# Attention scores from a stationary block that holds a query head's high part above its low part, in float32r, and two small tiles moved to another buffer ring

## The chip, the cores and the metric

The kernel runs on one core of a Trainium2 chip. The metric is device time in microseconds (us) of one execution. Engines are named as in the profile: PE (matrix multiply), DVE (vector), ACT (scalar and activation functions), POOL (GpSimd) and SP (here it only issues transfers). Each engine takes its instructions in the order of the program, and a transfer is issued when SP, POOL or ACT reaches it.

## The reference

Two layers over 256 latent tokens and 256 context tokens of width 1024. Each layer has a token mixer (windowed attention with grouped queries, and a recurrence in two directions called HGRN2, merged by gates and one output projection), then a mixture of experts in which each of 16 experts chooses its tokens. The change is in the scores of the attention:

```python
ATTN_HEADS = 8; ATTN_KV_HEADS = 2; HEAD_DIM = 64; WINDOW = 128; WBLOCK = 128
def window_attention(q, k, v, kc, vc, sink):       # latents: window keys and context keys
    ...
    s_win = jnp.einsum('bntgrd,bnsgd->bngrts', qb, kw).astype(jnp.float32) * scale
    ...
    s_ctx = jnp.einsum('bntgrd,bcgd->bngrtc', qb, kc).astype(jnp.float32) * scale
    ...
def context_attention(q, k, v, sink):              # context rows: context keys alone
    ...
    s = jnp.einsum('btgrd,bsgd->bgrts', qg, k).astype(jnp.float32) * (dh ** -0.5)
```

The latents' two blocks of 128 queries see 512 keys each (256 latents, of which the other block's are masked to the window, and 256 context tokens); the context's two blocks see 256. The context rows are needed in the first layer only. So there are 16 heads of scores against 512 keys and 16 against 256 in the first layer, and 16 against 512 in the second.

## The kernel before

The span has four stages: the mixer of layer 0 (until about 500 us), its experts (first expert at 534.67 us), the mixer of layer 1 (from about 976 us), and its experts (first expert at 1356.00 us, until the end). A framework's scheduler, which simulates the engines, fixes the order of instructions on every engine before the kernel runs. A tile that shares a buffer with an earlier one waits until the earlier one's last reader is done, so the buffers decide part of that order.

Mixers. The large products (input projections, branch products, output products) split each factor into a high and a low float32r part and add three products (`mm3`, L168 to L170); weights come by DMA (`win`, `wbr`, `wo`) and are split by ACT (L478) and by POOL or DVE (L479). Between them on PE stand the pieces of the attention and the recurrence. One head of scores was one float32 product: the stationary side is a query block `qT` of 128 rows (two heads of 64), the moving side is `kT`, four copies of the keys in which the other head's 64 rows are zero. `kT` is filled in `blk_ka` and zeroed in `kv_in`. Each head then goes through a chain of maximum, exponential, scaling, transposes and a product with the values (L704 to L727), on DVE, ACT and PE.

Fillers. The weights that turn the conditioning vector into scales and shifts are 80 tiles of 512 KB and some smaller ones. `mod_steps` makes them in steps: `load` issues a `wmod` transfer on SP (L284, two buffers), `work` multiplies it (four products, L294), and the eighth step of a group copies the result from PSUM to a row tile `mrow` (L247), transposes it (L250) and adds a bias (L254). The scheduler puts these steps into gaps.

Buffers. `T` has a ring of two [128, 512] buffers, taken by `t2(...)`, which small tiles of many kinds use one after the other: `qr`, `kr`, `vr`, `y`, `wraw` and, in the router, `wk`. `mrow` lay in the pool of the `wmod` tiles, of which the experts' pools (`moe_pools`) reuse the space, and the readout's tile `hg` (`hg_out`, L666) in the mixer's pool `C`.

Router. After a layer's mixer the post-norm, then `bcol` (DVE, L1045, after PE L1044), logits (PE L1065), softmax, and per row block `s` eight rounds of maximum and replace on `wk` (DVE, L1082 and L1083), which end in a one-hot tile `OH` (L1102). PE gathers the chosen rows by it (L1136), and the first expert follows (L1218). The experts' weights are 1 MB tiles on SP (L1011).

Of the kernel before, what the change touches and what calls it, by code (L numbers as in the profile page):

```python
# [11 lines left out]
F32 = mybir.dt.float32  # L12
# [97 lines left out]
def tile_kernel(ctx, tc, x, c, ctx_in, c_ctx, w_mod, b_mod, w_in, attn_sink, lb_fw, lb_bw, norm_g,  # L110
                w_br_a, w_br_h, w_out, w_router, w_gate, w_up, w_down, ln_g, ln_b, cst_d, msk_d, out):
    nc = tc.nc
# [165 lines left out]
    def mod_steps(l, q0, ns):  # L278

        state = {}  # L280

        def load(k, md):
            w = md.tile([128, 1024], F32, name="wmod", tag="wmod", bufs=2)
            ins = nc.sync.dma_start(w, _dram(w_mod, l * D * 6 * D + k * 128 * 6 * D + 512 * q0, [[6 * D, 128], [1, 1024]]))  # L284
            if first:
                in_order(first[:], ins)
            state[k] = w

        def work(k, md):
            if k == 0:  # L290
                state["p"] = mdb()
            pm, w = state["p"], state.pop(k)
            for j in range(4):
                mm(pm[32 * j:32 * j + 32, 0:256], scol[:, k, :], w[:, 256 * j:256 * j + 256],  # L294
                   start=(k == 0), stop=(k == KT - 1))
            if k < KT - 1:
                return
            mod_cols(l, pm, md.tile([128, 256], F32, name="mrow", tag="mrow", bufs=1), q0, 1, ns)
        return [(lambda md, k=k: load(k, md), lambda md, k=k: work(k, md)) for k in range(KT)]

    def mcol(l, sec, k, s):
# [122 lines left out]
    def front(l, fillers, X=None, finish=None):  # L424
# [229 lines left out]
        def hg_out(h, A, ihv):  # L654
            AT, A1, A2 = A
            p = ob()
            for t in range(NT):
                s, i = t // 2, t % 2
                terms = [(AT[:, t, :], t), (A1[:, s, i, :], 2 * s + 1 - i)]
                if s == 0:  # L660
                    terms += [(A2[:, j, 128 * i:128 * i + 128], 2 + j) for j in range(2)]
                for n, (a, tv) in enumerate(terms):
                    mm(p[:, 128 * t:128 * t + 128], a, ihv[:, tv, 128 * h:128 * h + 128], start=(n == 0),  # L663
                       stop=(n == len(terms) - 1), skip_group_check=True)
            pv = p[:, :TQ].rearrange("p (t v) -> p t v", v=128)
            hg = C.tile([128, TQ], F32, name="hg")  # L666
            nc.scalar.activation(hg, p[:, :TQ], AF.Square)
            r = T.tile([128, 4], F32, name="hr", tag="hr", bufs=2)[:, :NT]
            hg = hg.rearrange("p (t v) -> p t v", v=128)
            nc.vector.tensor_reduce(r, hg, axis=AX.X, op=ALU.add)  # L670
            nc.vector.tensor_scalar(r, r, 1.0 / 128, EPS, op0=ALU.mult, op1=ALU.add)
            nc.gpsimd.tensor_tensor(r, r, nhalf[:, 0:NT], op=ALU.pow)
            nc.vector.tensor_tensor(hg, pv, r[:, :, None].to_broadcast([128, NT, 128]), op=ALU.mult)
            for t in range(NT):
                nc.tensor.transpose(p[:, 128 * t:128 * t + 128], hg[:, t, :], ident)
            nc.vector.scalar_tensor_tensor(hgT[:, h, :], p[:, :TQ], ng[:, 4 * l + h:4 * l + h + 1], hgT[:, h, :],
                                           op0=ALU.mult, op1=ALU.mult)
# [11 lines left out]
        def attention(s, i2, qT, kT, va):  # L689
# [3 lines left out]
            t = 2 * s + i2  # L693
            tk = slice(128 * t, 128 * t + 128)
            for g in range(2):
                eT = C.tile([128, 4, 4, 128], F32, name="eT")
                for i in range(4):
                    hd = 4 * g + i
                    par = i % 2
                    p = scb()  # L700
                    mm(p[:, :nk], qT[:, hd // 2, tk], kT[:, 2 * g + par, k0:k0 + nk], start=True, stop=True)  # L701
                    if s == 0:
                        kc = 128 * (1 - i2)
                        nc.vector.tensor_tensor(p[:, kc:kc + 128], p[:, kc:kc + 128],  # L704
# [27 lines left out]
        def chains():  # L732
            nonlocal C, kT, va, ihv
            C = pool(sC, f"C{l}")
            kT = C.tile([128, 4, 512], F32, name="kT")
            va = C.tile([128, 4, 128], F32, name="va")
            ihv = C.tile([128, 4, 512], F32, name="ihv")

# [5 lines left out]
        def blk_ka(w, j):  # L744
            p = fm(w, j, 512)
            kr = t2("kr")
            rope(kr[:, 0:256], p[:, 0:256])
            nc.scalar.copy(kr[:, 256:512], p[:, 256:512])
            for g in range(2):
                for h in range(2):  # L750
                    (nc.scalar.copy if h else nc.vector.tensor_copy)(kT[64 * h:64 * h + 64, 2 * g + h, :],
                                                                     kr[64 * g:64 * g + 64, :])

        def blk_va(w, j):
            p = fm(w, j, 512)
# [38 lines left out]
            return A  # L794

        def kv_in():
            nc.gpsimd.memset(kT[64:128, 0:4:2, :], 0.0)
            nc.gpsimd.memset(kT[0:64, 1:4:2, :], 0.0)
            w = cols_tile((O_KA, 256))
            blk_ka(w, 0)  # L800
            blk_va(w, 1)
# [522 lines left out]
    def moe_pools(l, st, S, zones, right=()):  # L1324
# [5 lines left out]
        for z, names in enumerate((right,) + zones if right else zones):  # L1330
            Z = pool(sZ, f"ZR{l}", side="right") if names is right else pool(st, f"Z{l}{z}")
            for n in names:
                if isinstance(n, int):
                    for i in range(n):

                        w = 2304 if z == 2 + (right != ()) else 2048
                        slots.append(lambda Z=Z, i=i, w=w: Z.tile([128, w], F32, name=f"w{i}", tag=f"w{i}")[:, :2048])
                elif n not in shapes:

                    once.append(lambda Z=Z, n=n: Z.tile([128, 2048], F32, name="w" + n, tag=n))  # L1340
# [69 lines left out]
```

## Time and profile before

| | us |
|---|---|
| median of 3 runs | 1810.9 |
| lowest and highest | 1810.57, 1813.97 |
| profiled execution | 1812.94 |
| its span, first to last instruction | 1811.2 |
| PE, DVE, ACT, POOL busy in the span | 1562.6, 677.1, 450.0, 305.1 |
| mean granted clock of PE | 0.927 |

Busy times are sums over the span; what bounds a stage is read from the stage. In rows of the windows view each engine's figure is its busy time in that stretch with the number of its instructions behind it, then PE's granted clock, the share of the 16 DMA engines that was busy, and GB/s. In the chain of work each row is a start, a length, and the engine and line (or the DMA) that the end waited for.

### The profile page before, as it was taken

What the parts mean: (1) busy time and instruction counts of PE and PEld (TensorE: products, weight loads), DVE (VectorE), ACT (ScalarE), POOL (GpSimd) and SP (SyncE); (2) the same over time, 40 slices, a digit from 0 to 9 for tenths busy, and PEclk for the clock granted to TensorE, in tenths of its full rate; (3) what the DMA queues carried; (4) which work ended last, traced back from release to release, by engine and by line L of the source; (5) the groups of instructions that cost most, each with busy time, mean ns of one, the idle gap of its engine ahead of it and who ended that gap; (6) DMA issues with size and microseconds to landing.
All of it is one profiled execution on the core that took longest, in us unless ns stands there. A gap on an engine that the chain in (4) does not pass through costs nothing.

```text
span 1811.2 us, 27388 instructions
## 1 busy us (share of the span) xinstructions
PE 1562.6 (86%) x11342; PEld 925.0 (51%) x11342; DVE 677.1 (37%) x1430; ACT 450.0 (25%) x850; POOL 305.1 (17%) x302
## 2 busy tenths in 40 slices
PE   6999999999989999997998899998968766666666
PEld 4777776688754433332323788775845222322222
DVE  4546566323661221211213756666751100100102
ACT  2436556323120100101000533576410000000000
POOL 2342121123310000000002633331610000000001
PEclk9999999999979999999999999999979777867887
DMA  9644123533679999999999653424689999999997
GB/s 323 186 117 127 60 82 129 177 126 117 245 308 385 421 421 421 421 422 421 421 421 379 208 178 105 130 92 131 241 341 408 421 421 422 420 421 421 421 421 287
DMA packets 159436, 526.06 MB, mean 290 GB/s; under 512 B 9896, under 2 KB 94064, under 8 KB 111184
## 3 DMA queue, kind: packets, MB, share of 16 engines
q1 hardware_dynamic: 157136, 517.46, 74.1%
q0 software_dynamic: 1456, 4.49, 0.7%
q10 hardware_dynamic: 720, 2.36, 0.4%
q8 instruction: 89, 1.46, 0.3%
q14 instruction: 35, 0.29, 0.0%
HBM read 523.23 MB, written 1.05 MB: 289 GB/s over the span
## 4 chain that ended last, share of the span: by engine, by line
PE 53%; DMA 37%; DVE 4%; ACT 2%; POOL 2%; issue 1%; SPq 1%; POOLq 0%; ACTq 0%; DVEq 0%
DMA w<-in_w_up_dram 13%; DMA w<-in_w_down_dram 12%; PE acc L168 9%; DMA w<-in_w_gate_dram 9%; PE acc L170 8%; PE acc L169 8%; PE acc L1218 8%; PE o L1251 4%; DMA wmod<-in_w_mod_dram 3%; PE md L294 2%; PE sc L701 2%; PE sc L724 1%; PE o L663 1%; PE tr L719 1%; PE hs L649 1%
## 5 line engine op out<-in xcount | busy, mean ns | idle before, releaser
L1218 PE MATMUL acc<-w,xs 128*32 128x256 f32 (+1 forms) x3064 | 402.9, 512 | 92.0 <-DMA w<-in_w_up_dram 48.9
L1218 PEld LDWEIGHTS acc<-w,xs 128*32 128x32 f32 (+1 forms) x3064 | 138.0, 130 | 339.2 <-issue 175.9
L1251 PE MATMUL o<-w,hT 128*32 128x256 f32 (+1 forms) x1432 | 188.9, 507 | 44.9 <-DMA w<-in_w_down_dram 30.5
L168 PE MATMUL acc<-uTh,wh 128*128 128x512 f32 (+1 forms) x592 | 215.1, 365 | 3.0 <-ACT qr L682 1.3
L169 PE MATMUL acc<-uTl,wh 128*128 128x512 f32 (+1 forms) x592 | 212.0, 358 | 1.4 <-DVE uTl L398 1.4
L170 PE MATMUL acc<-uTh,wl 128*128 128x512 f32 (+1 forms) x592 | 210.1, 355 | 0.0
L1229 ACT ACTIVATE h<-acc 128x512 f32<-128x512 f32 (+1 forms) x32 | 15.7, 491 | 522.2 <-PE acc L1218 509.4
L479 POOL TENSOR_TENSOR wl<-win,wh 128x1024 fp32r<-128x1024 f32 x44 | 113.4, 2579 | 164.3 <-ACT wh L478 164.3
L1251 PEld LDWEIGHTS o<-w,hT 128*32 128x32 f32 (+1 forms) x1432 | 63.5, 130 | 149.0 <-issue 66.7
L1230 DVE TENSOR_TENSOR h<-h,acc 128x512 f32<-128x512 f32 (+1 forms) x32 | 17.7, 552 | 293.4 <-PE acc L1218 293.4
L168 PEld LDWEIGHTS acc<-uTh,wh 128*128 128x128 f32 x592 | 111.9, 190 | 28.0 <-issue 6.7
L169 PEld LDWEIGHTS acc<-uTl,wh 128*128 128x128 f32 x592 | 112.3, 190 | 18.3 <-issue 2.8
L170 PEld LDWEIGHTS acc<-uTh,wl 128*128 128x128 f32 x592 | 112.1, 189 | 17.6 <-issue 3.4
L478 ACT CAST wh<-win 128x1024 fp32r<-128x1024 f32 x84 | 84.0, 1047 | 88.0 <-PE acc L169 61.9
L1110 POOL TENSOR_TENSOR OW<-OH,aff 128x256 f32<-128x256 f32 x8 | 4.9, 616 | 583.9 <-PE sc L1233 569.0
L1274 DVE TENSOR_TENSOR Y<-o,g2 OH 32x512 f32<-32x512 f32 x60 | 41.2, 687 | 140.1 <-PE o L1251 139.3
L479 DVE TENSOR_TENSOR wl<-win,wh 128x1024 fp32r<-128x1024 f32 x40 | 51.7, 1294 | 84.8 <-ACT wh L478 84.6
L1235 ACT COPY hT<-sc 128x512 f32<-128x512 f32 (+1 forms) x32 | 15.3, 479 | 243.1 <-PE sc L1233 243.1
L1274 DVE TENSOR_TENSOR Y g<-o,Y g 32x256 f32<-32x256 f32 x60 | 25.2, 420 | 122.0 <-PE o L1251 121.3
L294 PE MATMUL md<-wmod,scol 128*32 128x256 f32 x640 | 59.0, 416 | 7.8 <-DMA wmod<-in_w_mod_dram 5.6
L564 DVE TENSOR_TENSOR K<-K,F 128x512 f32<-128x512 f32 x56 | 46.6, 832 | 8.9 <-PE hs L630 5.4
L333 POOL TENSOR_TENSOR mv<-mv,nhalf 128x1 f32<-128x1 f32 x26 | 24.4, 942 | 126.7 <-DVE mv L332 126.0
(450 smaller groups left out, 2373.3 us busy)
## 6 DMA issues: line engine op xcount, KB each, us to landing
w<-in_w_gate_dram SPq DMA_DIRECT2D x128, 1024.0 KB, 19.8
w<-in_w_up_dram SPq DMA_DIRECT2D x127, 1024.0 KB, 19.8
w<-in_w_down_dram SPq DMA_DIRECT2D x119, 1024.0 KB, 19.8
wmod<-in_w_mod_dram SPq DMA_DIRECT2D x80, 512.0 KB, 4.6
win<-in_w_in_dram SPq DMA_DIRECT2D x26, 1024.0 KB, 5.4
win<-in_w_in_dram SPq DMA_DIRECT2D x32, 512.0 KB, 5.3
wmod<-in_w_mod_dram SPq DMA_DIRECT2D x32, 256.0 KB, 5.9
wo<-in_w_out_dram SPq DMA_DIRECT2D x8, 1024.0 KB, 5.0
```

The costliest lines, as they stand in the source:

```text
L168: mm(p, a.hi, b.hi, start=start, stop=False, **kw)
L169: mm(p, a.hi, b.lo, start=False, stop=False, **kw)
L170: mm(p, a.lo, b.hi, start=False, stop=stop, **kw)
L294: mm(pm[32 * j:32 * j + 32, 0:256], scol[:, k, :], w[:, 256 * j:256 * j + 256], start=(k == 0), stop=(k == KT - 1))
L333: pows.append(nc.gpsimd.tensor_tensor(mv[:, 2:3], mv[:, 2:3], nhalf[:, 0:1], op=ALU.pow))
L478: nc.scalar.copy(hi[:, r], w[:, r])
L479: ins = eng.tensor_sub(lo[:, r], w[:, r], hi[:, r])
L564: nc.vector.tensor_tensor(kv, kv, _view(f, 0, [[nf + 1, 2], [2, nf // 2], [0, m]]), op=ALU.mult)
L701: mm(p[:, :nk], qT[:, hd // 2, tk], kT[:, 2 * g + par, k0:k0 + nk], start=True, stop=True)
L1218: ins = mm(p[MW * j:MW * j + MW, :NW], xs[:, k, e4, :], wrow(w, k)[:, NW * j:NW * j + NW], start=(k == 0), stop=(k == KT - 1))
L1251: mm(py[MW * dj:MW * dj + MW, :NW], hT[:, 128 * m + MW * j:128 * m + MW * j + MW], wrow(wd, kt)[:, NW * dj:NW * dj + NW], start=(kt == 0), ...
L1274: nc.vector.tensor_tensor(o, py[r:r + 32, :NW], g2[r:r + 32, NW * dj:NW * dj + NW], op=ALU.mult)
```

## The change

A new tile `QS` per block of 128 queries and key group holds four heads, each as a stationary block of 128 rows: 64 rows of the query's float32r part (ACT copies) and 64 rows of the remainder (DVE subtractions). `kT` becomes two float32r tiles, `kT.hi` and `kT.lo`, each with the same 64 rows twice, so that no zeros are needed. A head's scores are two float32r products into the same PSUM tile, one with `kT.hi` and one with `kT.lo`. `hg` and `mrow` go into the ring of `T`, and the weight slots of one zone of `moe_pools` become 2048 wide where they were 2304.

```diff
-            mod_cols(l, pm, md.tile([128, 256], F32, name="mrow", tag="mrow", bufs=1), q0, 1, ns)
+            mod_cols(l, pm, t2("mrow")[:, :256], q0, 1, ns)
...
-            hg = C.tile([128, TQ], F32, name="hg")
+            hg = t2("hg")[:, :TQ]
...
+                QS = C.tile([128, 4, 128], F32R, name="QS")
+                qs = QS.rearrange("p (i two) u -> p two i u", two=2)
+                for par in range(2):
+                    r, o = slice(64 * par, 64 * par + 64), slice(64 - 64 * par, 128 - 64 * par)
+                    qv = qT[r, 2 * g:2 * g + 2, tk]
+                    nc.scalar.copy(qs[r, par], qv)
+                    nc.vector.tensor_sub(qs[o, par], qv, qs[r, par])
...
-                    mm(p[:, :nk], qT[:, hd // 2, tk], kT[:, 2 * g + par, k0:k0 + nk], start=True, stop=True)
+                    mm(p[:, :nk], QS[:, i, :], kT.hi[:, g, k0:k0 + nk], start=True, stop=False)
+                    mm(p[:, :nk], QS[:, i, :], kT.lo[:, g, k0:k0 + nk], start=False, stop=True)
...
-            kT = C.tile([128, 4, 512], F32, name="kT")
+            kT = HL(*(C.tile([128, 2, 512], F32R, name="kT" + n) for n in "hl"))
...
+                r = slice(64 * g, 64 * g + 64)
                 for h in range(2):
-                    (nc.scalar.copy if h else nc.vector.tensor_copy)(kT[64 * h:64 * h + 64, 2 * g + h, :],
-                                                                     kr[64 * g:64 * g + 64, :])
+                    o = slice(64 * h, 64 * h + 64)
+                    nc.scalar.copy(kT.hi[o, g, :], kr[r, :])
+                for h in range(2):
+                    o = slice(64 * h, 64 * h + 64)
+                    nc.vector.tensor_sub(kT.lo[o, g, :], kr[r, :], kT.hi[r, g, :])
...
-            nc.gpsimd.memset(kT[64:128, 0:4:2, :], 0.0)
-            nc.gpsimd.memset(kT[0:64, 1:4:2, :], 0.0)
...
-                        w = 2304 if z == 2 + (right != ()) else 2048
-                        slots.append(lambda Z=Z, i=i, w=w: Z.tile([128, w], F32, name=f"w{i}", tag=f"w{i}")[:, :2048])
+                        slots.append(lambda Z=Z, i=i: Z.tile([128, 2048], F32, name=f"w{i}", tag=f"w{i}"))
```

The change also moves instructions, since the scheduler places them anew. Line numbers of the router grow by 11. Three places follow; the numbers behind the names tell tiles apart.

The first is PE where the first scores of layer 0 stand, between products of an input projection (L168 to L170). Before:

```order
L642 MATMUL hs_781<-Q_614,K_604 128x128 x4
L701 MATMUL sc_1403<-kT_601,qT_143 128x512
L701 MATMUL sc_1422<-kT_601,qT_143 128x512
L294 MATMUL md_1323<-wmod_1578,scol_77 32x256 x4
L168 MATMUL acc_1593<-uTh_144,wh_1587 128x512
```

And of the change:

```order
L642 MATMUL hs_782<-Q_615,K_605 128x128 x4
L709 MATMUL sc_1411<-kTh_601,QS_1405 128x512
L710 MATMUL sc_1411<-kTl_602,QS_1405 128x512
L709 MATMUL sc_1431<-kTh_601,QS_1405 128x512
L710 MATMUL sc_1431<-kTl_602,QS_1405 128x512
L294 MATMUL md_1326<-wmod_1599,scol_77 32x256 x4
L168 MATMUL acc_1614<-uTh_144,wh_1608 128x512
```

The place is the same; one float32 row per head became two float32r rows.

The second is PE in the router of layer 0, from the logits to the first expert. The last two `wmod` tiles of a filler group, whose products make the last `mrow`, stood behind the last logits (L1077 hands the softmax on to `wk`):

```order
L1077 MATMUL o_4670<-cst_67,aff_4627 16x128
L1070 MATMUL hs_4626<-cst_67,lT_4703 128x16
L1077 MATMUL o_4711<-cst_67,aff_4627 16x128
L294 MATMUL md_4408<-wmod_4443,scol_77 32x256 x4
L294 MATMUL md_4408<-wmod_4449,scol_77 32x256 x4
L1091 MATMUL tr_4622<-cst_67,wk_4524 128x16 x2
L250 MATMUL md_4457<-cst_67,mrow_4455 128x128 x2
L1136 MATMUL o_4733<-OH_4730,xh_4494 128x128 x8
```

Of the change, with L1055 the products that make `bcol` and L1076 the first logits:

```order
L1072 MATMUL sc_4652<-cst_67,xh_4569 128x128 x4
L1072 MATMUL sc_4663<-cst_67,xh_4569 128x128 x4
L294 MATMUL md_4483<-wmod_4518,scol_77 32x256 x4
L294 MATMUL md_4483<-wmod_4524,scol_77 32x256 x4
L250 MATMUL md_4532<-cst_67,mrow_4530 128x128 x2
L1055 MATMUL tr_4574<-modT0_108,wraw_4570 32x1 x16
L1076 MATMUL tr_4597<-u2_4616,oT_4550 32x128 x4
L1076 MATMUL tr_4597<-u2_4627,oT_4550 32x128 x4
```

The last two filler steps and their transposes moved from behind all logits to ahead of the first. On DVE the copy into `mrow` (L247) and L254 likewise stand right ahead of `bcol` now. On SP nothing moved there: the two `wmod` transfers still stand behind the second `w_down` pair.

The third is SP at the end of layer 1's mixer, where `wmod` are filler tiles, `wbr` and `wo` weights of the mixer and `w` weights of the experts. Before:

```order
L933 DMA wbr_9627<-in_w_branch_hgrn_dram 128x4x256
L284 DMA wmod_9635<-in_w_mod_dram 128x1024
L284 DMA wmod_9689<-in_w_mod_dram 128x1024
L284 DMA wmod_10034<-in_w_mod_dram 128x1024
L284 DMA wmod_10040<-in_w_mod_dram 128x1024
L284 DMA wmod_10046<-in_w_mod_dram 128x1024
L284 DMA wmod_10052<-in_w_mod_dram 128x1024
L1011 DMA w0_10254<-in_w_gate_dram 128x2048
```

Of the change:

```order
L944 DMA wbr_9887<-in_w_branch_attn_dram 128x4x256
L284 DMA wmod_9749<-in_w_mod_dram 128x1024
L967 DMA wo_9925<-in_w_out_dram 128x4x512
L284 DMA wmod_9803<-in_w_mod_dram 128x1024
L944 DMA wbr_9933<-in_w_branch_hgrn_dram 128x4x256
L284 DMA wmod_10148<-in_w_mod_dram 128x1024
L967 DMA wo_9982<-in_w_out_dram 128x4x512
L284 DMA wmod_10154<-in_w_mod_dram 128x1024
L967 DMA wo_9990<-in_w_out_dram 128x4x512
```

Before, the six last `wmod` of the layer stood together ahead of the first experts' weights. Now they stand behind the four `w_gate` tiles, in turn with the `wo` tiles of the output product, and their products on PE (L294) moved from the attention into the branch and output products.

## Rows read from the trace of the kernel before

**Rows 1.** Windows view, five stretches (PE, PEld, DVE, ACT, POOL).

```profile
200.00:290.00 90.00, 90.00 (x700) 67.63 (x699) 55.73 (x145) 57.30 (x119) 17.94 (x19) 1.00 0.26 83
...
290.00:390.00 100.00, 93.00 (x656) 64.57 (x655) 39.66 (x104) 40.27 (x88) 19.10 (x16) 0.97 0.50 164
...
700.00:950.00 250.00, 225.34 (x992) 78.11 (x990) 46.65 (x78) 17.11 (x34) 3.18 (x7) 0.99 1.01 421
...
1200.00:1270.00 70.00, 62.21 (x525) 43.15 (x524) 43.69 (x136) 46.28 (x100) 11.79 (x17) 0.95 0.39 126
```

**Rows 2.** Windows view, ten microseconds ahead of each layer's first expert.

```profile
530.00:540.00 10.00, 9.39 (x59) 5.77 (x60) 2.89 (x8) 3.90 (x7) 0.00 (x0) 1.00 0.24 79
1350.00:1360.00 10.00, 9.48 (x110) 7.69 (x113) 2.58 (x7) 3.45 (x6) 0.00 (x0) 0.82 0.25 82
```

**Rows 3.** Groups by line and shape on PE: scores (busy us, mean ns).

```profile
L701 PE MATMUL sc<-kT,qT 128*128 128x512 f32 x64 | 33.6, 620 | 0.0
...
L701 PE MATMUL sc<-kT,qT 128*128 128x256 f32 x32 | 10.4, 412 | 0.1
```

**Rows 4.** Chain of work, 285 to 350 us (start, length, what).

```profile
285.06 0.23 PE acc L168
...
306.83 4.99 DMA wmod<-in_w_mod_dram
...
322.82 0.43 PE sc L701 x2
...
336.65 7.03 DMA wmod<-in_w_mod_dram
```

**Rows 5.** Chain of work, 1195 to 1360 us.

```profile
1225.75 0.86 PE sc L701 x2
...
1227.31 0.12 PE acc L169
...
1234.82 4.91 DMA wmod<-in_w_mod_dram
...
1252.51 4.31 DMA wmod<-in_w_mod_dram
...
1310.36 11.22 DMA wraw<-in_w_router_dram
```

**Rows 6.** Instructions that touch the tile kT (ns: shortest, median, longest).

```profile
L751 DVE COPY kT<-kr x4: 420/421/423, 79.6 to 1150.5; 64x512 f32<-64x512 f32 x4
L751 ACT COPY kT<-kr x4: 616/618/620, 79.7 to 1151.8; 64x512 f32<-64x512 f32 x4
```

**Rows 7.** Groups on ACT: a copy of 64 rows by 256.

```profile
L633 ACT COPY AT<-hs 64x256 f32<-64x256 f32 x4 | 1.5, 364 | 2.3 <-PE hs L630 2.3
```

**Rows 8.** Timeline of SP, then the wmod transfers of 480 to 530 us.

```profile
502.10 0.80 SPq L284 DMA_DIRECT2D wmod<-in_w_mod_dram  x2
...
DMA to landing us min/median/max: 3.8/13.1/13.9
```

**Rows 9.** The page's DMA issues: the 512 KB wmod.

```profile
wmod<-in_w_mod_dram SPq DMA_DIRECT2D x80, 512.0 KB, 4.6
```

**Rows 10.** Timeline around layer 0's router.

```profile
503.62 0.15 DVE L1045 COPY bcol<-tr 128x2 f32<-128x2 f32 x1
...
520.21 1.93 PE L294 MATMUL md<-wmod,scol 128*32 128x256 f32 x16
...
523.94 0.39 DVE L1102 TENSOR_TENSOR OH<-cst,tr 128x256 f32<-128x256 f32 x1
...
530.10 0.42 DVE L1102 TENSOR_TENSOR OH<-cst,hs 128x256 f32<-128x256 f32 x1 [0.27 <-PE hs L1091]
```

**Rows 11.** Windows view of the router's stretch, then the tile X's instructions alone.

```profile
503.60:523.90 20.30, 13.56 (x115) 8.28 (x116) 17.46 (x59) 5.64 (x13) 3.01 (x5) 0.59 1.01 419
...
503.60:523.90 20.30, 0.00 (x0) 0.00 (x0) 5.44 (x7) 1.24 (x1) 0.00 (x0) 0.59 1.01 419
```

**Rows 12.** Chain of work, 470 to 540 us: the first expert.

```profile
534.67 5.72 PE acc L1218 x25
```

## The prediction

> **What bounds the kernel now.** I read the windows view by stage first. In the mixer of layer 0 PE is busy for the whole of 200 to 290 us while DVE and ACT are busy for some six tenths [rows 1]: there PE's order of work is the time, and a microsecond of PE taken out ends the stage a microsecond sooner. Behind it, from 290 to 390 us, PE has 7 us of gaps [rows 1]; the chain of work puts three waits for `wmod` transfers there, of 4.99 us for the first and 7.03 us for the last [rows 4]. In the end of layer 1's attention, 1200 to 1270 us, PE is busy for 62.21 of 70 us and DVE and ACT for over 40 each [rows 1]: that stretch is a chain through all of them, with three more `wmod` waits (4.91 the first, 4.31 the last) [rows 5]. The experts are bound by their weights: 700 to 950 us moves 421 GB/s with PE not full [rows 1]. But just ahead of the first expert the transfers run at 79 and 82 GB/s [rows 2], since all slots are full. So a shift of a layer's first expert shifts the stream of weights behind it and the end of the kernel by as much, and the question for each edit is when the first expert starts.
>
> **The scores.** The profile records a float32 product as two; 64 records against 512 keys and 32 against 256 [rows 3] are 32 and 16 heads. Their mean durations are pipelined and overlap, so I take the pace instead: a head against 512 keys takes 0.86 us of the chain and one against 256 takes 0.43 [rows 4, 5]. A float32r product of 512 columns takes 0.23 [rows 4], of 256 columns 0.12 [rows 5]. Two of them are 0.46 and 0.24, so a head saves 0.40 or 0.19. Layer 0: 16 x 0.40 + 16 x 0.19 = 9.4 us. Layer 1: 16 x 0.40 = 6.4 us. In layer 0 nearly all heads stand between dense products (the first place of the order), so I take 9.4 in full. In layer 1 I take half, 3.2: the heads before about 1200 us stand among dense products, those behind it in the chain, where ACT and DVE set much of the time.
>
> **What the scores cost elsewhere.** QS has 12 tiles (8 in layer 0, 4 in layer 1), each with two ACT copies and two DVE subtractions of 64 x 256: 24 and 24. An ACT copy of that shape takes 0.364 us [rows 7]; for DVE I take 0.42, that of its copy of 64 x 512 [rows 6], as an estimate. That is 16 x 0.364 = 5.8 us on ACT and 6.7 on DVE in layer 0, on engines with a third of the time free [rows 1]: nothing. In layer 1, 8 of each; a group's first head must wait for copy and subtraction in turn, some 0.8 us, four times at most: 0 to 3 us, of which I take 1. For kT, ACT makes four copies of 0.618 us per layer where it made two, and DVE four subtractions where it made two copies [rows 6]: 1.2 us more on ACT, and 0.8 to 2 on DVE, before the first scores and under the input projections; taken at nothing, at most 2 us if the first head comes to wait. The memsets that go were on POOL, on no chain.
>
> **Moved fillers, layer 0.** Five of the `wmod` tiles that were issued in the stretch with the gaps stand earlier now, under dense products; eight remain there. The gaps could shrink by up to their 7 us; but with the scores' PE work gone there is less to cover the rest, and SP still issues the remaining ones late. I take -0.5, from -7 to +6.
>
> **Moved fillers, layer 1.** Eight `wmod` tiles go behind the attention. The three waits there, from 4.91 to 4.31, are some 13.8 us, but PE fills most of such a wait with other work, since its idle time in the whole of 1200 to 1270 us is only 7.8 us [rows 1]. I take -5 for the attention. The tiles now stand on SP in turn with `wo` (the third place), and what waits on `wo` is behind them: I charge +3 for that, bounds 0 and +8. The chain's later part, with a wait of 11.22 us for the router's weights [rows 5], keeps its form; a POOL order with the last split ahead of that transfer is worth up to 2 us, which I take as 1. Layer 1 together: -3.2 + 1 - 5 + 3 - 1 = -5.2, between -12 and +3.
>
> **The router of layer 0.** This is the loss. `mrow` lies in the ring of T now, and `wk`, which the router needs for its first row block, comes behind it in the same ring. So the last two filler steps had to move ahead of the logits (the second place), on PE and on DVE, and both queues stop there until the two `wmod` tiles have landed. They are issued at 502.10 us and land 13.1 and 13.9 us later [rows 8], at about 516, whereas the middle one of all such transfers takes 4.6 [rows 9]: the experts' first weights, megabytes that were issued before, are still on their way. So `bcol`, which stood at 503.62 [rows 10], must wait for the landing, then for the products (1.93 us for sixteen records [rows 10]), the copy and the transposes: about 519.4. From `bcol` to the first one-hot the old order took 20.3 us with 17.46 of DVE, but 5.44 of that was on the tile X and is now done before `bcol` [rows 10, 11]. That leaves some 12 us of DVE and 2.8 of waits, or 14 to 17 with what the second row block puts between: 533.5 to 536.5. The second one-hot is then two to three microseconds behind, not six as before (530.10 after 523.94 [rows 10]), since both blocks' rounds run side by side: 536 to 539, where it was 530.10. The first expert, 534.67 before [rows 12], comes 5.5 to 9 us later. All of this moves with the scores' saving, since the issue of the transfers does. I take +7, with bounds of +4 (the weights ahead land sooner) and +11 (every step behind `bcol` finds its engine slow).
>
> The Trainium skill, "DMA: Bandwidth & Descriptors", section "Queues, rings and completion order", states that on each DMA engine descriptors are consumed in ring order. By that rule the two tiles cannot overtake the weights ahead of them, and the trace agrees with 13.1 and 13.9 us against 4.6; if they could overtake, they would be there before the logits, the term would be nothing, and the whole sum -15 instead of -8.
>
> **Sum.** -9.4 - 0.5 + 7 - 5.2 = -8.1 us against the profiled execution, which took 1812.94 us, 1.74 beyond its span. 1804.8; that execution lay 2.0 above the median of the runs shown, so as a median about 1802.8, called 1803. A change under 0.2% (3.6 us) can't be told from none here.
>
> **The rivals.**
> First, the scores pass in full and the router loses little, because the transfers land sooner or the wait hides behind the post-norm. Then the term of the router is 0 to 2, both layers give what their PE loses, and the waits in the gaps go as well: -9.4 - 4 + 2 - 10 = -21, about 1789.5. For it speaks that PE bounds layer 0; against it, that landing took 13 us.
> Second, no measurable change: the router takes +9 to +10, and in layer 1 the attention is set by maxima, exponentials and transposes, so that the shorter scores only lengthen PE's waits (0 to -2), the wmods' share being lost again at `wo`. -9.4 + 9.5 - 2 = -2, about 1809.
> Third, slower: the moved `wmod` tiles, which each engine meets in order, hold the end of layer 1. Three of the `wmod` tiles stand ahead of the three last `wo` tiles on SP and their buffers come free only when PE has done the products of earlier ones; a hold of a landing of 4.6 us [rows 9] for each `wo` would be up to 13.8 us, on top of which the router's +9: -9.4 + 9 - 3.2 + 1 - 5 + 13.8 = +6, about 1817. It decides from a hold of some 11.5 us on. Against it: PE has the output products of the earlier `wo` tiles to do while a later one comes.
> Fourth, the change doesn't do what it says: two float32r products at a pace of 0.43 each would save nothing. The dense products at 0.23 speak against it.
>
> **How the numbers follow.** My forecast (-14 to -4) 0.47; the first rival 0.19; no change 0.19; the third 0.13; the fourth 0.02, in effect no change or slower. The range takes in most of the first and the second and a part of the third: 1789 to 1815; the likeliest case alone is 1797 to 1807. Faster 0.65 (0.47 + 0.18), same 0.21, slower 0.14.
>
> **What would show it.** Scores: rows of L709 and L710 at a pace of 0.23 and 0.12, and the last output product of layer 0 some 10 us before its old time. Router: L294 ahead of the first logits with a wait on a `wmod` transfer, `bcol` 15 us behind the post-norm, the first expert of layer 0 only 2 to 4 us sooner than 534.67. Layer 1: no `wmod` wait between 1230 and 1260, `wmod` and `wo` waits in the output products. I am wrong if `bcol` comes before the tiles land, if layer 0 loses less than 8 us before its router, or if the output products of layer 1 wait more than they did.

## The result, and the profile after

The changed kernel takes 1835.2 us in the median of four runs against 1810.7 before, a ratio of 1.0135 with a 95% interval of 1.0123 to 1.0148: slower by 24.5 us, where 1803 was forecast. The profiled execution has a span of 1833.6 us against 1811.2.

Where the time went is read from the starts of a few instructions that both kernels have, taken from PE's timeline in each trace (us from the start of the span; each kernel's trace is of one execution, and those lie up to 3.4 us from the kernel's median, so a difference of a us or two between two starts can be chance):

| | first branch product, layer 0 | last output product | first expert | first branch product, layer 1 | last output product | first expert |
|---|---|---|---|---|---|---|
| before | 336.5 | 500.4 | 534.6 | 1266.3 | 1324.6 | 1355.9 |
| after | 331.4 | 499.2 | 547.9 | 1281.7 | 1348.5 | 1379.4 |
| difference | -5.2 | -1.2 | +13.3 | +15.4 | +23.9 | +23.5 |

So layer 0's mixer gains 1.2 us, its router loses 14.5, the way from there to layer 1's branch products loses 2.0, the branch and output products of layer 1 lose 8.5, and the rest gives back a little. The forecast was -9.9, +7 and -5.2 for layer 0, the router and layer 1, and the last three of these measured terms together make +10.2 for layer 1.

The scores do what the change says. The timeline of PE at the first heads of layer 0 (start, length, instruction; the lengths overlap, the starts give the pace):

```profile
129.36 0.48 PE L709 MATMUL sc<-kTh,QS 128*128 128x512 f32 x1
129.68 0.40 PE L710 MATMUL sc<-kTl,QS 128*128 128x512 f32 x1
129.91 0.39 PE L709 MATMUL sc<-kTh,QS 128*128 128x512 f32 x1
130.14 0.40 PE L710 MATMUL sc<-kTl,QS 128*128 128x512 f32 x1
```

The starts lie 0.23 us apart (0.32 behind the first), so a head takes 0.46 where the float32 one took 0.86 [rows 5]. The Trainium skill, "FP8 and Floating Point Precision", section "TensorE Precision Notes", states that true FP32 takes four passes through the PE array; if a float32r product is one pass, which that section doesn't say, the trace comes near it, 0.86 against 0.23 being 3.7. The added work has about the size that was estimated (an ACT copy takes 0.40 us, not 0.364), as the instructions on QS and kT in the trace of after show (ns: shortest, median, longest):

```profile
L702 ACT CAST QS<-qT x24: 389/403/407, 123.5 to 1252.2; 64x256 fp32r<-64x256 f32 x24
L703 DVE TENSOR_TENSOR QS<-qT,QS x24: 418/420/1062, 123.9 to 1253.3; 64x256 fp32r<-64x256 f32 x24
...
L765 DVE TENSOR_TENSOR kTl<-kr,kTh x8: 675/686/689, 80.3 to 1169.3; 64x512 fp32r<-64x512 f32 x8
```

What the scores save is there ahead of the stretch with the gaps. The last product of the input projection ahead of it starts 6.9 us sooner, as PE's timelines of before and of after show:

```profile
295.87 0.39 PE L168 MATMUL acc<-uTh,wh 128*128 128x512 f32 x1
```

```profile
289.02 0.39 PE L168 MATMUL acc<-uTh,wh 128*128 128x512 f32 x1
```

In the router of layer 0, PE's timeline of after:

```profile
499.18 0.40 PE L170 MATMUL acc<-wh,yinl 128*128 128x512 f32 x1
...
512.45 1.08 PE L294 MATMUL md<-wmod,scol 128*32 128x256 f32 x8 [9.80 <-DMA wmod<-in_w_mod_dram]
513.72 1.08 PE L294 MATMUL md<-wmod,scol 128*32 128x256 f32 x8 [0.19 <-DMA wmod<-in_w_mod_dram]
515.35 0.69 PE L250 MATMUL md<-cst,mrow 128*128 128x128 f32 x2 [0.55 <-DVE mrow L247]
...
517.10 0.60 PE L1055 MATMUL tr<-modT,wraw 128*32 128x1 f32 x30 [0.86 <-DMA wraw<-in_w_router_dram]
518.06 1.08 PE L1076 MATMUL tr<-u,oT 128*32 128x128 f32 x16 [0.36 <-POOL oT L1051]
```

The last output product starts at 499.18, and then PE stands for 9.80 us behind a `wmod` transfer, with the logits (L1076) behind it in the queue. The two transfers were issued at 500.87 and took, as the last line of the view of `wmod` says:

```profile
DMA to landing us min/median/max: 3.9/11.5/12.4
```

The forecast had 13.1 and 13.9 from [rows 8]. DVE's timeline of the same place:

```profile
509.14 0.81 DVE L347 TENSOR_SCALAR xh<-X,mv 128x1024 f32<-128x1024 f32 x1 [0.73 <-POOL mv L333]
514.87 0.43 DVE L247 COPY mrow<-md 128x256 f32<-128x256 f32 x1 [4.92 <-PE md L294]
516.07 0.37 DVE L254 TENSOR_TENSOR modT<-md,bmod 128x4 f32<-128x4 f32 x4 [0.78 <-PE md L250]
517.75 0.16 DVE L1056 COPY bcol<-tr 128x2 f32<-128x2 f32 x1 [1.31 <-PE tr L1055]
...
537.02 0.39 DVE L1113 TENSOR_TENSOR OH<-cst,tr 128x256 f32<-128x256 f32 x1
...
542.73 0.42 DVE L1113 TENSOR_TENSOR OH<-cst,hs 128x256 f32<-128x256 f32 x1 [0.54 <-PE hs L1102]
```

The wait that ends last ahead of `bcol` and the first logits is another one. The router's weights `wraw` take a place in the ring of T as well, and POOL issues their transfer at 509.65 where before issued it at 459.01. POOL's timelines, of before (L1034) and of after (L1045), have:

```profile
459.01 1.54 POOL L1034 DMA_DIRECT2D wraw<-in_w_router_dram  x2 [0.29 <-POOL wraw L1032]
```

```profile
509.65 1.57 POOL L1045 DMA_DIRECT2D wraw<-in_w_router_dram  x2 [0.30 <-POOL wraw L1043]
517.22 1.48 POOL L1051 TENSOR_TENSOR oT<-wraw,modT 128x128 f32<-128x128 f32 x4 [5.99 <-DMA wraw<-in_w_router_dram]
```

POOL waits 5.99 us for them, until 517.22, when the second `wmod` tile's products (513.72) are done. In runs 1 and 4 below, which have the last `mrow` in the ring, `wraw` is issued at 510.2 too; in all others but run 9 (494.0) at 450 to 462.

`bcol` stands at 517.75 (503.62 before [rows 10]), the one-hots at 537.02 and 542.73 (523.94 and 530.10 [rows 10]). From `bcol` to the first one-hot it takes 19.3 us, hardly less than the 20.3 of before. PE, waiting meanwhile, shows a granted clock of 0.50, its lower level of 1.2 GHz, from 530 to 540 us in the windows view:

```profile
530.00:540.00 10.00, 3.39 (x16) 2.91 (x16) 9.21 (x36) 0.36 (x2) 0.00 (x0) 0.50 0.00 1
```

Before shows that level in its router as well, so it is not what the change lost there:

```profile
510.00:520.00 10.00, 6.33 (x49) 4.22 (x42) 7.78 (x34) 1.68 (x7) 0.55 (x1) 0.50 1.02 416
```

At the end of layer 1's mixer the chain of work of after has

```profile
1301.28 8.55 DMA wo<-in_w_out_dram
1309.85 1.05 ACT wh L478
```

where the chain of before waits 5.02 us for a `wo`,

```profile
1297.26 5.02 DMA wo<-in_w_out_dram
```

and SP's timeline of after shows the transfer behind a `wmod`, and the next `wo` behind two more:

```profile
1300.77 0.34 SPq L284 DMA_DIRECT2D wmod<-in_w_mod_dram  x1
1301.28 1.22 SPq L967 DMA_DIRECT2D wo<-in_w_out_dram  x1
1302.60 0.44 SPq L284 DMA_DIRECT2D wmod<-in_w_mod_dram  x1
1305.83 0.37 SPq L944 DMA_DIRECT2D wbr<-in_w_branch_hgrn_dram  x1
1306.31 0.44 SPq L284 DMA_DIRECT2D wmod<-in_w_mod_dram  x1
1308.27 0.37 SPq L967 DMA_DIRECT2D wo<-in_w_out_dram  x1
```

In the mixer of layer 0, the filler products of after stand among the gate and branch products, as the groups by line on PE from 388 to 450 us show:

```profile
L294 PE MATMUL md<-wmod,scol 128*32 128x256 f32 x64 | 4.9, 390 | 0.0
```

In the same stretch of before there is no row of L294. The same holds from the first branch product to the last output product of layer 1: there too L294 has 64 records and 4.9 us in after and none in before. The windows view of PE alone, for that stretch of before and of after:

```profile
1266.30:1324.60 58.30, 53.12 (x339) 1.00 0.73 264
```

```profile
1281.70:1348.50 66.80, 59.41 (x409) 1.00 0.80 286
```

So of the 8.5 us lost there, 6.3 are more work of PE, most of it the moved fillers, and 2.2 are more idle time.

Ahead of it, from layer 1's first input product (1004.0 and 1019.3) to the first branch product, both kernels take the same time, 262.3 and 262.4 us, though PE's work fell by 5.9 us (250.84 to 244.93). The waits view of PE for these stretches shows what took its place: before waited 2.9 us for `wmod`,

```profile
PE md L294 <- DMA wmod<-in_w_mod_dram: 2.9, 5, 1.2
```

and after waits for no `wmod`, but longest for DVE and POOL in the recurrence:

```profile
PE hs L642 <- DVE AT L634: 6.5, 1, 6.5
PE hs L605 <- POOL KM L599: 3.9, 2, 3.0
```

### The profile page after: what moved, and what is told of

Read it like the earlier page. It is cut to its first block, busy times and chain, and to the rows that moved or that the text cites. A ratio compares the mean times of both kernels' runs of the same rounds, so it can differ in the third digit from the quotient of the medians.

```text
span 1833.6 us, 27446 instructions
## 1 busy us (share of the span) xinstructions
PE 1563.9 (85%) x11342; PEld 929.6 (51%) x11342; DVE 692.7 (38%) x1458; ACT 466.2 (25%) x882; POOL 302.5 (16%) x298
## 4 chain that ended last, share of the span: by engine, by line
PE 49%; DMA 39%; DVE 5%; ACT 3%; issue 2%; POOL 2%; SPq 0%; POOLq 0%; ACTq 0%; DVEq 0%
DMA w<-in_w_down_dram 12%; DMA w<-in_w_up_dram 12%; DMA w<-in_w_gate_dram 12%; PE acc L168 9%; PE acc L169 8%; PE acc L170 8%; PE acc L1229 7%; PE o L1262 3%; PE md L294 2%; PE sc L733 2%; DMA wmod<-in_w_mod_dram 1%; DMA win<-in_w_in_dram 1%; PE tr L728 1%; PE o L663 1%; PE hs L649 1%
## 5 line engine op out<-in xcount | busy, mean ns | idle before, releaser
L1262 PE MATMUL o<-w,hT 128*32 128x256 f32 (+1 forms) x1432 | 192.7, 525 | 37.8 <-DMA w<-in_w_down_dram 23.1
L168 PE MATMUL acc<-uTh,wh 128*128 128x512 f32 (+1 forms) x592 | 213.8, 363 | 2.9 <-ACT sgs L851 1.4
L170 PE MATMUL acc<-uTh,wl 128*128 128x512 f32 (+1 forms) x592 | 209.4, 354 | 0.0
L168 PEld LDWEIGHTS acc<-uTh,wh 128*128 128x128 f32 x592 | 111.7, 189 | 29.2 <-issue 8.3
L170 PEld LDWEIGHTS acc<-uTh,wl 128*128 128x128 f32 x592 | 111.8, 189 | 17.1 <-issue 3.0
L294 PE MATMUL md<-wmod,scol 128*32 128x256 f32 x640 | 57.2, 410 | 15.7 <-DMA wmod<-in_w_mod_dram 13.1
L564 DVE TENSOR_TENSOR K<-K,F 128x512 f32<-128x512 f32 x56 | 47.5, 848 | 14.8 <-PE hs L630 10.2
```

The costliest lines, as they stand in the source:

```text
L168: mm(p, a.hi, b.hi, start=start, stop=False, **kw)
L170: mm(p, a.lo, b.hi, start=False, stop=stop, **kw)
L564: nc.vector.tensor_tensor(kv, kv, _view(f, 0, [[nf + 1, 2], [2, nf // 2], [0, m]]), op=ALU.mult)
L1262: mm(py[MW * dj:MW * dj + MW, :NW], hT[:, 128 * m + MW * j:128 * m + MW * j + MW], wrow(wd, kt)[:, NW * dj:NW * dj + NW], start=(kt == 0), ...
```

## The experiments

The theory after the result: not the scores but the ring place of `mrow` makes the loss. The rival: the scores' copies and subtractions lengthen the attention. The experiments separate the edits, then the mechanisms. "mrow in its wmod tile" means that the copy goes into the first 256 columns of the last `wmod` tile of its group, whose products are done by then, so that it needs no place of its own.

**1. mrow in the ring alone.** The kernel before with

```diff
-            mod_cols(l, pm, md.tile([128, 256], F32, name="mrow", tag="mrow", bufs=1), q0, 1, ns)
+            mod_cols(l, pm, t2("mrow")[:, :256], q0, 1, ns)
```

and the 2048-wide slots, which runs 2 and 12 have as well.

> The kernel before with one edit of the change: mrow in the ring of T (and the 2048-wide slots). Scores and hg as before. Theory A (the loss is the ring place of mrow: layer 0's router waits for two wmod tiles, filler products move from the gap of layer 0 into its dense branch products, and wo in layer 1 waits behind wmod): slower than the change itself, since the scores' saving is missing: 1833 to 1845 us, first expert of layer 0 at 550 to 558. Theory B (the scores' extra ACT and DVE work lengthens the attention and costs most of the loss): only the router's 14 us, 1821 to 1828.

Measured: 1833.1 us, ratio 1.0119 (1.0103 to 1.0135). First expert of layer 0 at 547.3, layer 1's at 1375.1. This edit, without the scores, makes 22 of the change's 24.5 us; the slots alone don't: run 12 has them and loses 3.6. So with `mrow` in the ring the scores and `hg` together bring nothing (2 us more, within the two intervals), where without it the scores take off 10 (run 3). Theory A's time is met at its lower end, its first expert comes 3 us sooner than it said.

**2. hg in the ring, mrow in its wmod tile.** The kernel before with the 2048-wide slots and

```diff
-            mod_cols(l, pm, md.tile([128, 256], F32, name="mrow", tag="mrow", bufs=1), q0, 1, ns)
+            mod_cols(l, pm, w[:, 0:256], q0, 1, ns)
...
-            hg = C.tile([128, TQ], F32, name="hg")
+            hg = t2("hg")[:, :TQ]
```

> The kernel before with hg in the ring of T and mrow in the last wmod tile of its group (no ring place of its own, no extra space). Both theories: the time of before within 3 us, 1808 to 1814, and the first expert of layer 0 at 533 to 537; it is the base for the scores.

Measured: 1818.7 us, ratio 1.0039 (1.0026 to 1.0051), a loss that neither theory had. Run 12 splits it.

**3. The scores, mrow in its wmod tile.** The changed kernel with

```diff
-            mod_cols(l, pm, t2("mrow")[:, :256], q0, 1, ns)
+            mod_cols(l, pm, w[:, 0:256], q0, 1, ns)
```

> The changed kernel, with mrow in the last wmod tile of its group, so that the ring of T does not hold it; scores and hg as in the change. Theory A: filler products and router go back to the order of before, and the scores' saving shows: 1796 to 1804 us, first expert of layer 0 at 524 to 530. Theory B: 1815 to 1826.

Measured: 1809.1 us, ratio 0.9986 (0.9974 to 0.9998). First expert of layer 0 at 532.4. This is 26 us under the change, and 9.7 under its base, run 2: the scores save time and the rival B falls. But 1809 lies between the ranges of the two theories, and the first expert comes 2 us later than theory A said: the saving does not pass in full.

**4. The last mrow in the ring.** As run 3, but

```diff
+            mod_cols(l, pm, t2("mrow")[:, :256] if (l, q0) == (1, 2) else w[:, 0:256], q0, 1, ns)
```

> As the run before, but the last mrow ahead of layer 0's router alone is in the ring of T, so that its two filler steps stand ahead of the logits and nothing else moves. Theory A: 12 to 15 us above that run, 1809 to 1818, with bcol at some 508 to 518 behind the landing of two wmod tiles. Theory B says nothing else here; if the wait were hidden the two would be equal.

Measured: 1825.9 us, ratio 1.0078 (1.0065 to 1.0092). First expert 547.6 where run 3 has 532.4: 15.2 us from one tile's place, 16.9 in the medians.

**5. All but the last mrow in the ring.** The condition of run 4 the other way round.

> The changed kernel with the last mrow ahead of layer 0's router in its wmod tile and all other mrow in the ring of T: the filler products stay where the change put them, the router's order is that of before. If the loss is made of independent parts (the router some 15 us, the wo waits of layer 1 some 9, the fillers of layer 0 about nothing on balance): 15 us under the change and 9 to 12 over the version with no mrow in the ring, 1817 to 1822, first expert of layer 0 at 532 to 535, output products of layer 1 losing 7 to 10 us. If the router alone carries it: 1806 to 1812.

Measured: 1821.4 us, ratio 1.0061 (1.0044 to 1.0077). First expert of layer 0 at 532.9; from the first branch product to the last output product of layer 1 it takes 67.2 us, where before took 58.3 and run 3 takes 58.0. The parts nearly add up: 16.9 (run 4 over run 3) and 12.3 (run 5 over run 3) are 29, and the change lies 26 over run 3.

**6 and 7. No filler loads, with the old and the new scores.** In runs 2 and 3, `mod_steps` loads its tile once per layer and multiplies it every time:

```diff
-            w = md.tile([128, 1024], F32, name="wmod", tag="wmod", bufs=2)
-            ins = nc.sync.dma_start(w, _dram(w_mod, ...))
+            if id(md) not in once_w:
+                once_w[id(md)] = md.tile([128, 1792], F32, name="wmod", tag="wmod", bufs=1)
+                ins = nc.sync.dma_start(once_w[id(md)][:, 0:1024], _dram(w_mod, ...))
...
+            state[k] = once_w[id(md)]
```

`mrow` has a tile of its own there. Of 80 transfers of 512 KB two are left (the 112 in the expectation counts 32 others, of the first scales, which stay; so some 41 MB are left out, not 50).

> Float32 scores, hg in the ring, and the wmod tiles of mod_steps loaded once per layer instead of 112 times, so that all scales and shifts but the first are of the wrong weights: this leaves out 50 MB of transfers and keeps all products. It is the base for the next run. The end of layer 0's attention should come 6 to 12 us sooner than in before if the transfers set its pace there, and the whole be 1780 to 1805 us.

> As the run before, with the scores of the change. Theory C (layer 0's saving of 8 us is there at 190 us and is swallowed by the wmod transfers at 296 to 340 us): without these transfers the saving reaches the branch products, 6 to 9 us of it, and the first branch product comes that much sooner than in the run before; in all 8 to 14 us under it. Theory D (the saving is swallowed by the chain of DVE, ACT and PE of the recurrence and the attention, whatever the transfers): no more than 3 us of it arrives there.

Measured: 1819.7 (ratio 1.0051, 1.0037 to 1.0065) and 1808.9 us (0.9990, 0.9981 to 0.9999). The base missed its expectation: with the old scores the gap of layer 0 ends no sooner than in before, and 1.3 us sooner than in run 2. The pair answers the question all the same. The first and last start of the first branch products (L168), in runs 2 and 3, and then in 6 and 7:

```profile
L168 PE MATMUL acc<-ah0h,wh x64: 278/388/497, 338.4 to 1299.6; 128*128 128x512 f32 x32, 128*128 128x256 f32 x32
```

```profile
L168 PE MATMUL acc<-ah0h,wh x64: 278/390/664, 336.3 to 1293.5; 128*128 128x512 f32 x32, 128*128 128x256 f32 x32
```

```profile
L168 PE MATMUL acc<-ah0h,wh x64: 278/380/794, 337.1 to 1301.8; 128*128 128x512 f32 x32, 128*128 128x256 f32 x32
```

```profile
L168 PE MATMUL acc<-ah0h,wh x64: 277/389/793, 330.9 to 1292.2; 128*128 128x512 f32 x32, 128*128 128x256 f32 x32
```

With loads the new scores bring the branch products from 338.4 to 336.3, 2.1 us; without, from 337.1 to 330.9, 6.2 us, and the first expert 8.0 us sooner (534.0 to 526.0) where with loads it was 4.5 (536.9 to 532.4). Theory C holds for most of it: the transfers swallow what the scores save. SP's timeline of run 3 shows how:

```profile
299.56 45.28 SPq L284 DMA_DIRECT2D wmod<-in_w_mod_dram  x15
```

Fifteen tiles through two buffers take 45.28 us, 3.0 each. In before, the same row (from 305.62, 39.14 us, 13 tiles) has the same pace, and in run 2 (from 304.10, 43.06 us, 14 tiles) too. So with the new scores this row begins 4.5 us sooner and has a tile more to bring at 3 us: it ends 2.3 us sooner, about what the branch products gain.

The end of the kernel does not follow. With the new scores the first expert of layer 0 comes 6.4 us sooner without the loads (532.4 to 526.0), but the first branch product of layer 1 only 1.4 us sooner (1264.6 to 1263.2), and the medians are the same (1809.1 and 1808.9). What holds layer 1's attention there is not shown.

**8. The scores without the rings.** Run 3 with `hg` in C and, to fit, in layer 1

```diff
-                QS = C.tile([128, 4, 128], F32R, name="QS")
+                    QS = C.tile([128, 4 // nq, 128], F32R, name="QS")
...
-                    qv = qT[r, 2 * g:2 * g + 2, tk]
+                        qv = qT[r, 2 * g + j:2 * g + j + 2 // nq, tk]
```

with `nq` 2 in layer 1, made ahead of the first and the third head.

> Scores of the change alone: hg in the pool C as before, mrow in its wmod tile; to fit, QS of the second layer holds two heads and is made twice per group. If hg in the ring costs what the run with hg and mrow in wmod lost over before (7 us), then 1800 to 1805 us, the fastest so far; if that loss came of mrow in wmod, 1807 to 1812.

Measured: 1815.9 us, ratio 1.0035 (1.0024 to 1.0046), a miss. The first expert of layer 0 comes at 530.9, the soonest with all loads (run 10, whose edits agree in layer 0, has 532.0, so chance makes a us of it), but layer 1's branch products only at 1268.6 (1264.6 in run 3). The second half of QS stands in one buffer behind the first half's scores. I take that for the loss; it is argued, not shown.

**9. The change without filler loads.** The edit of run 7 in the changed kernel, `mrow` in the ring.

> The change with all mrow in the ring of T, but the wmod tiles of mod_steps loaded once per layer, so that later scales and shifts are of the wrong weights; the order of PE in layer 0's router stays (last filler products and transposes ahead of bcol and the logits). If the late landing of the wmod tiles makes the router's loss and the wo waits: 18 to 26 us under the change, within 3 us of the kernel with new scores and no filler loads (1806 to 1815), first expert at 525 to 530, no wo loss. If the order alone costs (products, copy and transposes ahead of bcol on PE and DVE): first expert no sooner than 536, 1818 to 1826.

Measured: 1821.1 us, ratio 1.0052 (1.0035 to 1.0069), 14 under the change, and the first expert at 534.8: between the two. Its DVE timeline:

```profile
497.84 0.42 DVE L247 COPY mrow<-md 128x256 f32<-128x256 f32 x1
...
505.08 0.88 DVE L350 TENSOR_SCALAR xh<-X,mv 128x1024 f32<-128x1024 f32 x1 [0.73 <-POOL mv L336]
505.88 0.14 DVE L1059 COPY bcol<-tr 128x2 f32<-128x2 f32 x1
...
524.29 0.39 DVE L1116 TENSOR_TENSOR OH<-cst,tr 128x256 f32<-128x256 f32 x1
```

No `wmod` transfer is waited for, and still `bcol` comes 11 us behind the last output product (494.8), since DVE's order has the whole post-norm up to `xh` ahead of it; before it came 3.2 us behind (503.6 and 500.4). From the last output product to the first expert it takes 40.0 us, where before took 34.2, run 7 takes 32.7 and the change 48.7. So of the router's loss over the same scores without the ring (48.7 - 32.7 = 16), 8.7 goes with the late landings and 7.2 stays with the order. The 8.7 are not those of the `wmod` tiles alone: without them POOL's order also has `wraw` sooner, issued at 494.0 where the change issues it at 509.65, and no run takes the two apart.

**10 and 11. hg out of the ring in another way.** Run 3 with `hg` in C in layer 0, and in layer 1 in the ring `tp` (run 10) or `te` (run 11):

```diff
+            hg = (tp("hg")[:, :TQ] if last else C.tile([128, TQ], F32, name="hg"))
```

> Scores of the change, mrow in its wmod tile, hg in the pool C in layer 0 as before and in the one-buffer ring tp in layer 1, so that QS holds four heads and neither ring place of the change is used. From the parts so far (hg in the ring of T loses some 2 us in layer 0 and 3 to 4 in layer 1): 1801 to 1806 us. If QS itself is what loses at the end of layer 1's attention: 1808 to 1814.

> As the run before with hg of layer 1 in the ring te, which the attention's exponentials use: 1802 to 1810 us; slower than with tp if the exponentials wait for it.

Measured: 1808.5 us, ratio 0.9978 (0.9964 to 0.9992), and 1827.3, ratio 1.0086 (1.0072 to 1.0101). Run 10 has the lowest median here, 0.2% under before, but its interval overlaps that of run 3 (0.9974 to 0.9998), so it is not shown to be faster than that run. It misses the first expectation by 2 us and lies in the second, that QS itself loses at the end of layer 1's attention; the run moves `hg` too, so that this is not shown. Run 11 is slower by far more than expected: layer 1's branch products start at 1281.5, 16 us later than in run 10, in the ring that the exponentials use.

**12. mrow in its wmod tile alone.** The kernel before with the first edit of run 2 and the 2048-wide slots.

> The kernel before with mrow in its wmod tile alone; scores and hg as before. If hg in the ring made the 7 us of the run with both: 1808 to 1813 us, equal to before. If holding a wmod buffer for mrow costs: 1815 to 1820.

Measured: 1814.9 us, ratio 1.0018 (1.0009 to 1.0027), in the gap between the two expectations: about half of run 2's loss (3.6 of 7.4 us) is this, the other half `hg`.

**13. No filler loads in layer 1.** Run 5 with the edit of run 7 for the mixer of layer 1 alone.

> As the run in which all but the last mrow are in the ring (1821 us, 8 us lost in the branch and output products of layer 1), with the wmod tiles of layer 1's own mixer loaded once only, so that its later scales and shifts are of the wrong weights; layer 0 is untouched. If the loss there is the wo transfer that lands late behind wmod tiles: 5 to 9 us less, 1812 to 1816, and no gap between the two products. If it is the place of mrow between the y tiles in the ring, or of the filler products: the loss stays, 1819 to 1823.

Measured: 1815.2 us, ratio 1.0019 (1.0009 to 1.0029), 6.2 under run 5. From the first branch product to the last output product 61.4 us, against 67.2 in run 5 and 58.3 before: of 8.9 lost, 5.9 goes with the transfers and 3.1 stays with the order. The moved products are still there, and PE is busy for 59.28 of 61.3 us: without the loads they fill waits that PE had in before, with them they come on top.

## Why the prediction was wrong

Three terms of the sum failed: layer 0's saving (-9.9 forecast, -1.2 measured), the router (+7, 14.5) and layer 1 (-5.2, +10.2), which miss by 8.7, 7.5 and 15.4 us, all to the same side. Two of the three signs of being wrong that were named came: layer 0 lost less than 8 us before its router, and the output products of layer 1 waited more.

- **What bounds the stages** was read rightly where the router was concerned: the first expert's delay went through to the end, 13.3 us of it at layer 0. That a shift of the first expert always shifts the end by as much is not so: in run 7, which leaves out the loads of both layers, it came 6.4 us sooner than in run 3, and the end did not. Layer 0's mixer was read wrongly, below.
- **The scores' price** was right: 0.46 us per head, and copies and subtractions of 0.40, 0.42 and 0.69 us on ACT and DVE.
- **The step "so I take 9.4 in full" failed.** Some 7 us of it were there at the end of the dense products (6.9 in the change, 7.0 from run 2 to run 3, 6.7 from run 6 to run 7) and were swallowed by the gap behind them, which is paced by `wmod` tiles at 3 us each. Runs 2, 3, 6 and 7 show it: 2.1 us arrive at the branch products with the transfers, 6.2 without. In the order of the change even less arrives, 0.2 us from run 1 (331.5) to the change (331.4); without the loads (run 9) its branch products come at 327.1, 4.2 us sooner, so there the transfers hold a part, and the share of the chain through ACT and DVE is not shown. I had these waits in [rows 4] and treated them as a term of their own, when they were the limit of the first term: work saved ahead of a chain that is paced by transfers only lengthens the wait there.
- **The step "-0.5" for layer 0's fillers** had a range that held the truth, but its reason was the wrong way round: I wrote that five tiles stand earlier now; the trace shows 64 records of L294 (eight tiles) among the gate and branch products, behind the gap. The gap ends 5 us sooner, with the new scores or without (331.4 and, in run 1, 331.5), and PE pays that back in a stretch where it is the limit, down to 1.2 us at the last output product.
- **The router's term was mis-sized:** +7, bounds 4 to 11, measured 14.5 from the last output product to the first expert, in which the shift of the whole is already taken out. `bcol` came about where it was put (519.4 forecast, 517.75 measured with a shift of -1.2), and this is in part luck: the `wmod` tiles landed a little sooner than forecast, and the wait for `wraw`, which the forecast did not have, ended last. The miss lies behind `bcol`. "14 to 17" us from there to the first one-hot came from DVE's busy time, when the chain through PE, ACT and DVE takes 19.3 even with the post-norm out of the way; run 9, with no `wmod` landing to wait for, has 18.4. The second one-hot was put two to three microseconds behind the first and came 5.7 behind, another 3 us: its transpose (L1102) stands on PE behind 26 records of the first block's gather, which this row of after's PE timeline shows

```profile
537.46 3.79 PE L1147 MATMUL o<-OH,xh 128*128 128x128 f32 x16 [0.71 <-DVE OH L1113]
541.04 1.42 PE L1147 MATMUL acc<-OH,xh 128*128 128x128 f32 x10
542.39 0.29 PE L1102 MATMUL hs<-cst,wk 16*128 16x16 f32 x2
```

- **Layer 1's term failed in sign:** -5.2 forecast, +10.2 measured between the first experts (23.5 - 13.3). The charge of +3 for `wo` was 8.5, just beyond its bound of 8. It counted a wait on `wo` alone and put the moved fillers' own time on PE at nothing: PE does 6.3 us more work in the branch and output products, where it had 5.2 us idle. The third rival's mechanism, moved `wmod` tiles that hold `wo`, is there as well: run 13 gives 5.9 us to the transfers. The 5 us for the waits taken out of the attention, and the scores' 3.2, did not arrive: 2.0 us more than before from the first expert to the branch products. The `wmod` waits went as forecast, but PE itself had stood only 2.9 us for them, and waits for DVE and POOL in the recurrence came in their place (6.5 and 3.9 us). Which edit orders these so stays open; from the first expert to the branch products run 2 takes 2.0 us more than before, run 8 5.9 and run 11 17.6, each with small tiles placed in another way.
- **The rivals.** The third, slower, was the right side, at 1817; neither it nor the range reached 1835. Its 9 us for the router were nearer than my 7, its 13.8 for `wo` no nearer to 8.5 than my 3, and it kept the -9.4 for the scores.
- The Trainium skill, "DMA: Bandwidth & Descriptors", section "Queues, rings and completion order", states that on each DMA engine descriptors are consumed in ring order; after agrees with it as well, with 11.5 and 12.4 us to landing behind the expert weights.

## What to carry to other kernels

Ask of a small tile's ring what comes behind it there: here one [128, 256] tile, moved to save 1 KB per partition, tied a step that nothing needed soon to the router's critical path and cost 16.9 us there (run 4 over run 3) and 21.8 in all its places (run 1), where the faster scores save 9.7 (run 3 under run 2). Work that is moved out of a wait costs its own time where it goes. A saving on a busy engine counts up to the next stretch that is paced by something else; follow it to there before adding it up. And a tile that is dead anyway (here the last weight tile) may hold the small one, at a cost of 0.2% here.

## What was not expected

- Taking out 78 transfers of 512 KB left the time where it was (1818.7 and 1819.7 us with the old scores, 1809.1 and 1808.9 with the new), though three of them stood in the chain of layer 0. With the old scores the branch products of layer 0 came only 1.3 us sooner: the limits lay within a few us of each other. With the new ones they came 5.4 us sooner, which layer 1 lost again.
- Moving one tile of 1 KB per partition changed the time by 17 to 22 us three times (run 1 over before, run 4 over run 3, run 11 over run 10), where the whole change of arithmetic gave 10 (run 3 under run 2).
